# Weight-block sums by accumulating DMA, and a rearranged end, in an encoder layer on one NeuronCore

## Chip, cores, metric

One core of a Trainium2 chip runs one encoder layer for two request groups. The metric is the time of one execution on the device in microseconds (us); lower is better. Three runs of the kernel before are the base.

## Reference

```python
def encoder_trunk(x, mem, ...):          # prompt: 512 tokens, sample: 1024 tokens, D = 1024
    x = layer_norm(x, ln_in_g, ln_in_b)
    x = layer_norm(ALPHA * x + token_mixer(x, ...), ln1_g, ln1_b)
    x = layer_norm(ALPHA * x + memory_cross_attention(x, mem, ...), ln2_g, ln2_b)
    x = layer_norm(ALPHA * x + squared_relu_mlp(x, w_up, w_down), ln3_g, ln3_b)
    return x

def squared_relu_mlp(x, w_up, w_down):   # w_up: 1024 x 4096, w_down: 4096 x 1024
    return jnp.square(jax.nn.relu(x @ w_up)) @ w_down
```

All is float32. The change lies in the MLP of the two groups, in the norm behind it, and in nothing ahead of it.

## The kernel before

Every float32 product is made of three matmuls: an operand is split into a rounded high part (a copy on ACT into float32r) and the rest (a subtraction on GpSimd or DVE), and high x high, high x low, low x high are added in PSUM. `V`, `A`, `G`, `T`, `S` are the queues of DVE (VectorE), ACT (ScalarE), GpSimd (POOL), TensorE and SP, which issues all DMAs. A scheduler orders each queue when the program is built; buffers come from rings (`SLOT`: `qt`, `pt`, `gb`, `kv` two of 128x1024 each, `q` seven of 128x512, `cpr` two; `wh` and `wl` three of 128x1024 each; `act` six of 128x4096), so a load waits until the tile that held its buffer is used up.

**MLP of the prompt.** 32 steps f. Each loads 128 columns of `w_up` and 128 rows of `w_down` (`col_block`, `down_weights`), splits them (ACT, GpSimd), makes the hidden block (`up`: 24 matmuls, relu, square, split) and adds its product with the `w_down` rows to the four token tiles (`down`: 24 matmuls, eight DVE additions from PSUM). Beside it `left` makes ready, for the sample group, the left operands of the next stage: four blocks per product, each a sum or difference of two blocks of the activations or one alone, split and stored to `sa` in DRAM.

**MLP of the sample group.** Both matrix products are done as 2 x 2 blocks with seven products instead of eight (Strassen). `PRODUCTS[i]` names for each product its left blocks, its right (weight) blocks and where the result is added or subtracted; `UP` and `DOWN` are the orders of the seven. A step of an up product (16 a product) loads one or two 128x512 weight blocks (`up_block`, 256 KB each), combines two of them on DVE into `cpr`, splits (`right`, with the subtraction on GpSimd here), does 12 matmuls and adds the bank to one or two hidden blocks. `left_load` fetches a product's four left tiles from `sa` some half a product ahead. A step of a down product combines and splits a hidden block (left) and a `w_down` block (right), both subtractions on DVE, and does 12 matmuls for four token tiles; behind a product its four banks are added to the accumulators `accs`. `finish(0)` normalizes the upper 512 rows behind product 1, `finish(1)` the lower 512 behind the last product:

```python
        if i == 1:
            finish(0)
    finish(1)
```

Of the kernel before, what the change touches and what calls it, by code (L numbers as in the profile page):

```python
# [36 lines left out]
def tile_encoder_layer(ctx: ExitStack, tc: tile.TileContext, d, outs):  # L37
# [818 lines left out]
    for t in range(4):  # L856
# [16 lines left out]
    UP, DOWN = (5, 3, 2, 4, 1, 7, 6), (3, 5, 4, 2, 7, 1, 6)  # L873


    def left(i):
        blk = lambda b, k: X2[1 + b[0]][:, 4 * b[1] + k]
        what = PRODUCTS[i][0]
        for k in range(4):
            x = blk(what[0], k)  # L880
            if len(what) > 1:
                y = slot("cpr")
                V.tensor_tensor(y, x, blk(what[2], k), op=what[1])
                x = y
            t = slot("kv", dt=F32R)
            A.activation(t[:, 0:512], x, AF.Copy)
            V.tensor_sub(t[:, 512:1024], x, f32(t[:, 0:512]))
            S.dma_start(sa[i - 1][k], f32(t).rearrange("p (j c) -> p j c", j=2))
# [65 lines left out]
    def right(what, load, low, tag=None):  # L954
# [75 lines left out]
    for n, i in enumerate(DOWN):  # L1030
# [33 lines left out]
        if i == 1:  # L1064
            finish(0)
# [65 lines left out]
```

## Time and profile before

| | us |
|---|---|
| median of three runs (2437.79 to 2443.6) | 2439.3 |
| the profiled execution | 2432.93 |
| its span, first to last instruction | 2431.2 |
| TensorE busy | 2321.2 (95%) |
| MLP of the prompt, first to last `down` addition (L925) | 1415.8 to 1773 |
| up products, sample | about 1780 to 2086 |
| down products, sample | 2086 to 2412 |

The chip's profiler records each instruction with its engine and line; "PE" is TensorE, "DVE" VectorE, "ACT" ScalarE, "POOL" GpSimd. PEclk is the share of TensorE's full clock that was granted. A wait is put down to the instruction that ended last before it. Window rows read: stretch, its length, then busy us and (x count) of PE, PEld (weight loads), DVE, ACT and POOL, then PEclk, the mean busy share of the 16 DMA engines, and GB/s.

### The profile page before, as it was taken

How to read it: one execution, taken by the hardware profiler on the slowest of the kernel's cores; microseconds unless marked ns; L12 is line 12 of the kernel's file. 1: busy time of each engine (PE TensorE's matmuls, PEld its weight loads, DVE VectorE, ACT ScalarE, POOL GpSimd, SP SyncE). 2: the span in 40 equal slices, each digit the busy share in tenths (PEclk: the TensorE clock that was granted, in tenths of full speed). 3: DMA queues.
4: the chain of work that ended last, by engine and by line, in shares of the span. 5: the costliest groups of instructions: out<-in, count | busy, mean ns of one | idle time of the engine just before them, and what ended most of it. 6: DMA issues, size and time to landing. Idle time of an engine off the chain costs nothing.

```text
span 2431.2 us, 33241 instructions
## 1 busy us (share of the span) xinstructions
PE 2321.2 (95%) x11128; PEld 1916.6 (79%) x11128; DVE 1667.1 (69%) x3294; ACT 1034.1 (43%) x2181; POOL 910.0 (37%) x798
## 2 busy tenths in 40 slices
PE   8989999999999999999989989999999999999995
PEld 6868778898888787778878876788888877888873
DVE  6266545666656776658576679666655799887997
ACT  4346644666545634434233334333354222344432
POOL 7555442121234125333244444454475445100013
PEclk9999999999999999999999999999999999999998
DMA  9676345444444543435325366433376677634553
GB/s 323 199 191 174 85 119 131 118 115 101 94 119 116 168 130 104 139 113 173 108 92 188 101 205 242 131 98 93 100 242 180 192 240 219 208 125 147 189 170 119
DMA packets 394043, 371.00 MB, mean 153 GB/s; under 512 B 72976, under 2 KB 302352, under 8 KB 393872
## 3 DMA queue, kind: packets, MB, share of 16 engines
q1 hardware_dynamic: 393872, 368.88, 50.7%
q8 instruction: 88, 1.44, 0.2%
q14 instruction: 83, 0.68, 0.1%
HBM read 290.75 MB, written 52.97 MB: 141 GB/s over the span
## 4 chain that ended last, share of the span: by engine, by line
PE 38%; DVE 9%; DMA 4%; issue 3%; POOL 2%; ACT 1%; POOLq 0%; SPq 0%; DVEq 0%; ACTq 0%
PE pj L128 5%; PE pj L129 5%; PE pj L130 5%; DVE cpr L960 2%; PE s L128 2%; PE s L130 2%; PE s L129 2%; PE t L128 2%; PE t L130 2%; PE t L129 2%; PE t L1045 1%; PE t L1046 1%; PE t L1047 1%; DVE h L1001 1%; DMA q<-in_w_up_dram 1%
## 5 line engine op out<-in xcount | busy, mean ns | idle before, releaser
L106 POOL TENSOR_TENSOR wl<-wraw,wh 128x512 fp32r<-128x512 f32 x144 | 196.6, 1378 | 262.8 <-ACT wh L105 240.3
L960 DVE TENSOR_TENSOR cpr<-q 128x512 f32<-128x512 f32 x160 | 148.8, 931 | 47.4 <-DMA q<-in_w_up_dram 19.2
L155 POOL TENSOR_TENSOR lnst<-lnst,mhalf 128x1 f32<-128x1 f32 x48 | 51.6, 1078 | 342.5 <-DVE lnst L154 339.6
L432 ACT ACTIVATE q<-q,st 128x256 f32<-128x256 f32 (+3 forms) x256 | 138.2, 545 | 74.9 <-DVE st L431 72.0
L963 ACT ACTIVATE wh<-cpr 128x512 fp32r<-128x512 f32 x160 | 100.3, 627 | 161.5 <-DVE cpr L960 140.2
L105 ACT ACTIVATE wh<-wraw 128x512 fp32r<-128x512 f32 x144 | 87.9, 629 | 182.3 <-DMA wraw<-in_w_up_dram 50.3
L478 DVE TENSOR_TENSOR pt<-t,pt 128x512 fp32r<-128x512 f32 x160 | 105.4, 671 | 86.5 <-ACT pt L477 85.9
L964 POOL TENSOR_TENSOR wh<-cpr,wh 128x512 fp32r<-128x512 f32 x80 | 114.4, 1431 | 115.7 <-ACT wh L963 115.7
L296 POOL TENSOR_TENSOR wl<-wraw,wh 128x256 fp32r<-128x256 f32 x128 | 95.5, 771 | 153.5 <-ACT wh L295 141.8
L912 POOL TENSOR_TENSOR wl<-wraw,wh 128x512 fp32r<-128x512 f32 x64 | 87.4, 1378 | 122.4 <-ACT wh L911 122.3
L477 ACT ACTIVATE pt<-t 128x512 fp32r<-128x512 f32 x160 | 89.5, 583 | 87.9 <-PE o L490 84.6
L490 PE MATMUL o<-pt,tok 128*128 128x256 f32 (+3 forms) x560 | 114.3, 315 | 5.7 <-ACT q L496 4.3
L925 DVE TENSOR_TENSOR tok<-tok,s 128x512 f32<-128x512 f32 x124 | 83.5, 681 | 41.1 <-PE s L130 41.0
L118 POOL TENSOR_TENSOR wl<-wraw,wh 128x512 fp32r<-128x512 f32 x48 | 62.9, 1324 | 124.9 <-ACT wh L117 124.7
L128 PE MATMUL pj<-x20h,wh 128*128 128x512 f32 x256 | 102.1, 399 | 7.1 <-ACT wh L105 7.0
L925 DVE TENSOR_TENSOR tok<-tok,t 128x512 f32<-128x512 f32 x124 | 83.1, 682 | 31.7 <-PE t L130 31.6
L130 PE MATMUL pj<-x20h,wl 128*128 128x512 f32 x256 | 102.1, 399 | 2.2 <-POOL wl L106 2.1
L129 PE MATMUL pj<-x20l,wh 128*128 128x512 f32 x256 | 101.7, 397 | 0.0
L1040 ACT ACTIVATE wh<-wraw 128x512 fp32r<-128x512 f32 x80 | 50.6, 633 | 119.0 <-issue 40.8
L474 PE MATMUL t<-ident,q 128*128 128x128 f32 x624 | 94.9, 274 | 2.2 <-DVE pt L478 1.0
L490 PEld LDWEIGHTS o<-pt,tok 128*128 128x128 f32 x560 | 83.5, 192 | 11.3 <-ACT q L496 6.2
L428 DVE CUSTOM_DVE_ANT_0 q<-s,gb 128x256 f32<-128x256 f32 (+2 forms) x160 | 67.9, 466 | 27.4 <-PE s L449 21.6
(478 smaller groups left out, 7545.3 us busy)
## 6 DMA issues: line engine op xcount, KB each, us to landing
q<-in_w_up_dram SPq DMA_DIRECT2D x192, 256.0 KB
q<-in_w_down_dram SPq DMA_DIRECT2D x192, 256.0 KB
wraw<-in_w_in_dram SPq DMA_DIRECT2D x96, 256.0 KB
wraw<-in_w_up_dram SPq DMA_DIRECT2D x64, 256.0 KB
wraw<-in_w_down_dram SPq DMA_DIRECT2D x64, 256.0 KB
sa<-kv SPq DMA_DIRECT2D x28, 512.0 KB
kv<-in_c_rope_dram SPq DMA_DIRECT2D x24, 512.0 KB
hd<-qt SPq DMA_DIRECT2D x96, 128.0 KB
```

Of the source, the lines that this page charges most:

```text
L106: G.tensor_sub(wl[:, sl], r, f32(wh[:, sl]))
L128: T.matmul(out, lh[k], rh[k], start=(k == 0), stop=False, skip_group_check=True)
L129: T.matmul(out, lh[k], rl[k], start=False, stop=False, skip_group_check=True)
L130: T.matmul(out, ll[k], rh[k], start=False, stop=(k == n - 1), skip_group_check=True)
L296: G.tensor_sub(dl, src, f32(dh))
L432: A.activation(p, p, AF.Exp, bias=nm, accum_out=den)
L478: V.tensor_sub(lo[:, 0:x], t[:, 0:x], f32(hi[:, 0:x]))
L490: T.matmul(o[:, q0:q0 + n], v(c, h), part[:, x:x + n], start=(done == 0 and part is hi), stop=(done == total - 1 and part is lo), skip_gro ...
L925: V.tensor_add(x, x, q)
L960: V.tensor_tensor(y, x, z, op=what[1])
L963: A.activation(t[:, 0:512], x, AF.Copy)
L964: low.tensor_sub(t[:, 512:1024], x, f32(t[:, 0:512]))
```

## The change

Four parts. (1) Where a product's two weight blocks are added, `right` loads the first into a `q` buffer through SP and lets GpSimd issue a second DMA that adds its block to that buffer; the DVE addition goes. Signs in `PRODUCTS` are changed so that all right operands but product 1's are sums (its difference stays on DVE, L970 in the new file). In the up products the split's subtraction goes from GpSimd to DVE (L964, L976 in the new file). (2) `left` works on one block a step in 28 steps instead of four in 7, and the prompt's MLP loads whole 512 KB tiles of weights into `qt` and `pt`. (3) `DOWN` becomes (3, 5, 4, 7, 1, 6, 2). The last product goes over tokens 0 to 383 first (three banks) and keeps its weight splits in `act` buffers (`kept`), then over the last 128 tokens. (4) The upper rows' statistics are taken behind products 5 and 1, and their norms stand inside the last product's loop; the lower rows' norms follow their banks tile by tile.

```diff
-    def layer_norm(x, g, b, spread=0):
+    def layer_norm(x, g, b, spread=0, st=None):
-        st = sb.tile([P, 16], F32, name="lnst", bufs=2)
-        V.bn_stats(st[:, 0:6], x[:, 0:512])
-        V.bn_stats(st[:, 6:12], x[:, 512:1024])
+        if st is None:
+            st = sb.tile([P, 16], F32, name="lnst", bufs=2)
+            V.bn_stats(st[:, 0:6], x[:, 0:512])
+            V.bn_stats(st[:, 6:12], x[:, 512:1024])
...
-        3: (((0, 0),), ((0, 1), SUB, (1, 1)), (((0, 1), ADD), ((1, 1), ADD))),
+        3: (((0, 0),), ((0, 1), ADD, (1, 1)), (((0, 1), ADD), ((1, 1), ADD))),
...
-    UP, DOWN = (5, 3, 2, 4, 1, 7, 6), (3, 5, 4, 2, 7, 1, 6)
+    UP, DOWN = (5, 3, 2, 4, 1, 7, 6), (3, 5, 4, 7, 1, 6, 2)
...
     def down_weights(f):
         hi, lo = (x.rearrange("p (j c) -> p j c", j=2) for x in w_parts())
+        raw = w_raw(wdn[f * P:(f + 1) * P].rearrange("p (j c) -> p j c", j=2), "pt")
         for ch in range(2):
-            raw = w_raw(wdn[f * P:(f + 1) * P, None, ch * 512:(ch + 1) * 512])[:, 0]
-            A.activation(hi[:, ch], raw, AF.Copy)
-            G.tensor_sub(lo[:, ch], raw, f32(hi[:, ch]))
+            A.activation(hi[:, ch], raw[:, ch], AF.Copy)
+            G.tensor_sub(lo[:, ch], raw[:, ch], f32(hi[:, ch]))
...
-        w, dn = col_block(wup, f * P), down_weights(f)
+        w, dn = col_block(wup, f * P, "qt"), down_weights(f)
         down(up(w), dn, f == 0)
-        if 3 <= f < 10:
-            left(UP[f - 3])
+        if 3 <= f < 31:
+            left(UP[(f - 3) // 4], (f - 3) % 4)
...
+    def transfer(out, src, onto):
+        if onto is None:
+            S.dma_start(out, src)
+        else:
+            G.dma_start(out, src, accum_op=ADD)
...
         x = load(what[0])
-        if len(what) > 1:
+        if len(what) > 1 and what[1] == ADD:
+            load(what[2], x)
+        elif len(what) > 1:
             z = load(what[2])
             y = slot("cpr")
             V.tensor_tensor(y, x, z, op=what[1])
             x = y
...
-            wh_, wl_ = (x.rearrange("p (k c) -> p k c", k=4) for x in right(what, up_block(f), G))
+            wh_, wl_ = (x.rearrange("p (k c) -> p k c", k=4) for x in right(what, up_block(f), V))
...
+    def left_parts(lw, c, t0, t1):
+        n = (t1 - t0) * P
+        x = hidden(lw[0], c)[:, t0 * P:t1 * P]
+        if len(lw) > 1:
+            y = wp.tile([P, 512], F32, name="wraw", tag="wraw", bufs=2)[:, 0:n]
+            V.tensor_tensor(y, x, hidden(lw[2], c)[:, t0 * P:t1 * P], op=lw[1])
+            x = y
+        a = wp.tile([P, 1024], F32R, name="wh", tag="wh")
+        A.activation(a[:, 0:n], x, AF.Copy)
+        V.tensor_sub(a[:, 512:512 + n], x, f32(a[:, 0:n]))
...
+    for n, i in enumerate(DOWN[:-1]):
...
+        if i in (5, 1):
+            for t in range(4):
+                stats(0, t, 1 if i == 5 else 0)
...
+    for c in range(16):
+        if c % 8 == 0:
+            kept.append([act.tile([P, 8, 512], F32R, name="kept", tag="act") for _ in range(2)])
+        rs = right(rw, down_block(c), V, dst=[k[:, c % 8] for k in kept[c // 8]])
+        chunk(banks[0:3], left_parts(lw, c, 0, 3), rs, c)
+        if c % 4 == 3:
+            finish(0, c // 4, 1)
+    for t in range(3):
+        collect(into, t, banks[t])
+    for c in range(16):
+        chunk(banks[3:4], left_parts(lw, c, 3, 4), [k[:, c % 8] for k in kept[c // 8]], c)
+    for t in range(4):
+        if t == 3:
+            collect(into, 3, banks[3])
+        finish(1, t, 2 if t == 3 else 1)
```

Up to the prompt's MLP every queue stands as before. Three places behind that show what moved. The first is DVE's queue in the middle of the burst of `left` before (L883 combines two blocks, L887 is a split's subtraction into `kv`, L925 an addition to a token tile, L901 and L904 belong to `up`):

```order
L901 TENSOR_TENSOR cpr<-cpr 128x512
L887 TENSOR_TENSOR kv<-cpr,kv 128x512
L904 TENSOR_TENSOR q<-cpr,q 128x512
L925 TENSOR_TENSOR tok<-tok,s 128x512
L887 TENSOR_TENSOR kv<-xt_13867,kv 128x512
L883 TENSOR_TENSOR cpr<-xt_12957,xt_13867 128x512
L887 TENSOR_TENSOR kv<-xt_13867,kv 128x512
L901 TENSOR_TENSOR cpr<-cpr 128x512
L925 TENSOR_TENSOR tok<-tok,t 128x512
L925 TENSOR_TENSOR tok<-tok,s 128x512
L925 TENSOR_TENSOR tok<-tok,t 128x512 x2
L887 TENSOR_TENSOR kv<-xt_13867,kv 128x512
```

and the same queue in a step of the change (the lines are now L884, L888, L926, L902, L905):

```order
L884 TENSOR_TENSOR cpr<-xt_12957,xt_13867 128x512
L926 TENSOR_TENSOR tok<-tok,s 128x512
L926 TENSOR_TENSOR tok<-tok,t 128x512
L902 TENSOR_TENSOR cpr<-cpr 128x512
L926 TENSOR_TENSOR tok<-tok,s 128x512
L888 TENSOR_TENSOR kv<-cpr,kv 128x512
L905 TENSOR_TENSOR q<-cpr,q 128x512
L926 TENSOR_TENSOR tok<-tok,s 128x512
```

Four splits for `kv` among a few additions have become one among a step's additions.

The second is GpSimd's queue from the end of the prompt's norms through all products of the sample group, before (L155 and L170 are norms, L964 the splits' subtractions; `qt` are upper rows):

```order
L170 TENSOR_TENSOR tok<-tok,gb 128x1024
L964 TENSOR_TENSOR wh<-q,wh 128x512 x4
L964 TENSOR_TENSOR wh<-cpr,wh 128x512 x16
L964 TENSOR_TENSOR wh<-q,wh 128x512 x16
L964 TENSOR_TENSOR wh<-cpr,wh 128x512 x64
L155 TENSOR_TENSOR lnst<-lnst,mhalf 128x1 x2
```

and now (L960 issues an accumulating DMA, L157 and L172 are norms):

```order
L960 DMA q<-in_w_up_dram 128x4x128
L172 TENSOR_TENSOR tok<-tok,gb 128x1024
L960 DMA q<-in_w_up_dram 128x4x128 x62
L960 DMA q<-in_w_down_dram 128x512 x60
L157 TENSOR_TENSOR st<-st,mhalf 128x1 x4
L960 DMA q<-in_w_down_dram 128x512 x4
L172 TENSOR_TENSOR qt<-qt,q 128x512 x2
```

All subtractions have left this queue, and 128 DMAs stand in it, the last four of them behind the upper rows' first norm operations.

The third is DVE's queue at the end. Before, the last banks (L1057) and the lower rows' norms follow the last split (L964):

```order
L964 TENSOR_TENSOR wh<-cpr,wh 128x512
L1057 TENSOR_TENSOR gb<-gb,pj 128x512 x2
L152 BN_STATS lnst<-gb 128x6
L1057 TENSOR_TENSOR kv<-kv,s 128x512 x2
L152 BN_STATS lnst<-gb 128x6
L153 BN_AGGR lnst<-lnst 128x2 x2
L154 TENSOR_SCALAR lnst<-lnst 128x1
L159 SCALAR_TENSOR_TENSOR gb<-gb,lnst,g_21726 128x512 x2
```

Now the first three tiles' banks (L1072) and norms (L153 to L161) stand among the second pass's small combinations and splits (L1052, L1056):

```order
L1056 TENSOR_TENSOR wh<-wraw,wh 128x128
L1052 TENSOR_TENSOR wraw<-tok,h_17336 128x128
L1072 TENSOR_TENSOR gb<-gb,pj 128x512 x4
L1072 TENSOR_TENSOR kv<-kv,s 128x512 x2
L153 BN_STATS lnst<-gb 128x6
L1056 TENSOR_TENSOR wh<-wraw,wh 128x128
L154 BN_STATS lnst<-gb 128x6
L1056 TENSOR_TENSOR wh<-wraw,wh 128x128
L153 BN_STATS lnst<-gb 128x6
L154 BN_STATS lnst<-gb 128x6
L1052 TENSOR_TENSOR wraw<-tok,h_17336 128x128
```

Three of the four lower tiles are now collected and normalized ahead of the last matmuls, not behind them.

## Rows read from the trace of the kernel before

**Rows 1.** The page: TensorE's busy time, its share of the span, instructions.

```profile
PE 2321.2 (95%) x11128; PEld 1916.6 (79%) x11128; DVE 1667.1 (69%) x3294; ACT 1034.1 (43%) x2181; POOL 910.0 (37%) x798
```

**Rows 2.** Windows: MLP burst, MLP later, up twice, down twice, after the last matmul.

```profile
1440.00:1530.00 90.00, 77.21 (x302) 59.16 (x301) 77.09 (x107) 38.45 (x65) 38.05 (x26) 0.92 0.71 248
1600.00:1760.00 160.00, 160.00 (x697) 130.24 (x696) 102.24 (x146) 51.41 (x86) 78.07 (x58) 1.00 0.33 98
1780.00:1940.00 160.00, 160.00 (x700) 131.20 (x699) 96.36 (x123) 68.83 (x120) 92.31 (x64) 1.00 0.70 210
1940.00:2060.00 120.00, 114.11 (x484) 92.41 (x484) 115.48 (x130) 25.54 (x41) 59.30 (x41) 0.97 0.77 230
2060.00:2340.00 280.00, 279.61 (x1230) 230.42 (x1229) 244.39 (x385) 114.52 (x196) 10.04 (x6) 1.00 0.53 172
2340.00:2412.00 72.00, 57.30 (x230) 44.41 (x228) 62.01 (x107) 24.66 (x40) 20.61 (x8) 0.95 0.38 128
2412.00:2431.20 19.20, 0.00 (x0) 0.00 (x0) 13.22 (x28) 4.11 (x6) 9.81 (x8) 0.63 0.27 109
```

**Rows 3.** Waits from 1390 to 1530 us: total us, times, longest.

```profile
ACT wh L105 <- DMA wraw<-in_w_up_dram: 20.2, 14, 3.8
ACT kv L886 <- DMA sa<-kv: 18.9, 14, 4.1
...
PE pj L128 <- ACT wh L105: 6.9, 3, 5.4
```

**Rows 4.** The chain that ended last, from 1700 us: start, us, what.

```profile
2009.35 1.79 DVE cpr L960
2012.38 1.78 DVE cpr L960
...
2129.97 0.68 PE t L1045 x3
2132.69 0.68 PE t L1045 x3
...
2305.04 0.68 PE t L1045 x3
```

**Rows 5.** Lines L960 and L964: count, ns of one (least/median/most), first and last start.

```profile
L960 DVE TENSOR_TENSOR cpr<-q x160: 665/691/1793, 1794.4 to 2403.1; 128x512 f32<-128x512 f32 x160
...
L964 POOL TENSOR_TENSOR wh<-cpr,wh x80: 1278/1298/1806, 1803.2 to 2075.6; 128x512 fp32r<-128x512 f32 x80
```

**Rows 6.** Windows in an up and a down product; SP's issue of up blocks.

```profile
1912.00:1948.00 36.00, 34.63 (x153) 28.39 (x152) 35.62 (x45) 6.96 (x11) 14.24 (x11) 1.00 0.59 171
2132.00:2168.00 36.00, 36.00 (x161) 29.80 (x160) 30.12 (x49) 15.15 (x26) 0.00 (x0) 1.00 0.40 125
...
L971 SPq DMA_DIRECT2D q<-in_w_up_dram x192: 367/430/1977, 1753.6 to 2065.8; - x192
```

**Rows 7.** Waits of TensorE from 2085 to 2431 us, the longest.

```profile
PE pj L1046 <- DVE wh L964: 13.8, 8, 4.3
```

**Rows 8.** Timeline of the end: start, us, engine, line, operation, count.

```profile
2411.56 0.39 PE L1047 MATMUL s<-wh 128*128 128x512 f32 x1
...
2412.43 1.26 DVE L1057 TENSOR_TENSOR kv<-kv,s 128x512 f32<-128x512 f32 x2
...
2418.49 0.69 DVE L151 BATCH_NORM_STATS2 lnst<-kv 128x6 f32<-128x512 f32 x1
...
2419.09 0.68 DVE L152 BATCH_NORM_STATS2 lnst<-kv 128x6 f32<-128x512 f32 x1
...
2422.55 1.41 DVE L159 SCALAR_TENSOR_TENSOR kv<-kv,lnst,g 128x512 f32<-128x512 f32 x2
...
2424.54 0.69 DVE L168 TENSOR_TENSOR kv<-kv,g 128x512 f32<-128x512 f32 x1
```

**Rows 9.** Line L170, GpSimd's bias additions of the last norms: count, ns of one.

```profile
L170 POOL TENSOR_TENSOR pt<-pt,g x2: 4859/6048/7237, 2382.3 to 2387.1; 128x512 f32<-128x512 f32 x2
L170 POOL TENSOR_TENSOR gb<-gb,g x2: 1262/1536/1809, 2417.9 to 2419.7; 128x512 f32<-128x512 f32 x2
```

More of the change, by code (lines that the diff above doesn't have):

```diff
@@ L872, in tile_encoder_layer, with left @@
     }
-    UP, DOWN = (5, 3, 2, 4, 1, 7, 6), (3, 5, 4, 2, 7, 1, 6)
-    def left(i):
-        blk = lambda b, k: X2[1 + b[0]][:, 4 * b[1] + k]
+    UP, DOWN = (5, 3, 2, 4, 1, 7, 6), (3, 5, 4, 7, 1, 6, 2)
+    def left(i, k):
+        blk = lambda b: X2[1 + b[0]][:, 4 * b[1] + k]
         what = PRODUCTS[i][0]
-        for k in range(4):
-            x = blk(what[0], k)
-            if len(what) > 1:
[L882 to L888, printed above, removed]
+        x = blk(what[0])
+        if len(what) > 1:
+            y = slot("cpr")
+            V.tensor_tensor(y, x, blk(what[2]), op=what[1])
+            x = y
+        t = slot("kv", dt=F32R)
+        A.activation(t[:, 0:512], x, AF.Copy)
+        V.tensor_sub(t[:, 512:1024], x, f32(t[:, 0:512]))
+        S.dma_start(sa[i - 1][k], f32(t).rearrange("p (j c) -> p j c", j=2))
     toks[0] = [slot("tok") for _ in range(4)]
@@ L961, in right, with load @@
             x = y
[L962 to L965 removed]
+        if dst is None:
+            t = wp.tile([P, 1024], F32R, name="wh", tag=tag or ("wh", "wl")[next(ring) % 2])
+            dst = t[:, 0:512], t[:, 512:1024]
+        A.activation(dst[0], x, AF.Copy)
+        low.tensor_sub(dst[1], x, f32(dst[0]))
+        return dst
     def up_block(f):
[L968 to L969 removed]
+        def load(b, onto=None):
+            r = slot("q", 512) if onto is None else onto
             c0 = b[1] * 2048 + f * P
[L971 to L972 removed]
+            transfer(r.rearrange("p (k c) -> p k c", k=4),
+                     wup[b[0] * 512:(b[0] + 1) * 512, c0:c0 + P].rearrange("(k p) c -> p k c", p=P), onto)
             return r
@@ L1013, in down_block, with load @@
     def down_block(c):
-        def load(b):
-            r = slot("q", 512)
+        def load(b, onto=None):
+            r = slot("q", 512) if onto is None else onto
             row = b[0] * 2048 + c * P
-            S.dma_start(r, wdn[row:row + P, b[1] * 512:(b[1] + 1) * 512])
+            transfer(r, wdn[row:row + P, b[1] * 512:(b[1] + 1) * 512], onto)
             return r
@@ L1021, in tile_encoder_layer, with stats, finish, chunk @@
     done = set()
-    g3 = None
-    def finish(h):
-        for t in range(4):
-            layer_norm(accs[h][t], [g3[:, 0], g3[:, 1]], [g3[:, 2], g3[:, 3]], 1 if t % 2 else 2)
-            row = 512 * h + t * P
-            S.dma_start(outs[1][0, row:row + P], accs[h][t])
-    for n, i in enumerate(DOWN):
+    stat = {}
+    def stats(h, t, ch):
+        if (h, t) not in stat:
+            stat[h, t] = sb.tile([P, 16], F32, name="st", bufs=4)
+        V.bn_stats(stat[h, t][:, 6 * ch:6 * ch + 6], accs[h][t][:, ch * 512:(ch + 1) * 512])
+    def finish(h, t, spread):
+        layer_norm(accs[h][t], g3, b3, spread, stat.get((h, t)))
+        row = 512 * h + t * P
+        S.dma_start(outs[1][0, row:row + P], accs[h][t])
+    def left_parts(lw, c, t0, t1):
[4 more added lines that the diff above has]
+            V.tensor_tensor(y, x, hidden(lw[2], c)[:, t0 * P:t1 * P], op=lw[1])
+            x = y
+        a = wp.tile([P, 1024], F32R, name="wh", tag="wh")
+        A.activation(a[:, 0:n], x, AF.Copy)
+        V.tensor_sub(a[:, 512:512 + n], x, f32(a[:, 0:n]))
+        return [(a[:, j * P:(j + 1) * P], a[:, 512 + j * P:512 + (j + 1) * P]) for j in range(t1 - t0)]
+    def chunk(banks, ls, rs, c):
+        for o, (lh, ll) in zip(banks, ls):
+            T.matmul(o, lh, rs[0], start=(c == 0), stop=False)
+            T.matmul(o, lh, rs[1], start=False, stop=False)
+            T.matmul(o, ll, rs[0], start=False, stop=(c == 15))
+    def collect(into, t, o):
+        for b, op in into:
+            x = accs[b[0]][t][:, b[1] * 512:(b[1] + 1) * 512]
+            if (b, t) not in done:
+                done.add((b, t))
+                V.scalar_tensor_tensor(x, x, ALPHA, o, op0=ALU.mult, op1=op)
+            else:
+                V.tensor_tensor(x, x, o, op=op)
+    for n, i in enumerate(DOWN[:-1]):
         lw, rw, into = PRODUCTS[i]
```

60 lines of the change are left out of this document (16 added, 44 removed).

## Prediction

> **What bounds the kernel now.** I read the page first: TensorE is busy 95% of 2431.2 us [rows 1], so an engine that is merely slow costs nothing; only the places where TensorE loses matmuls count. The busy figure hides them, because a matmul at a lower clock is also busy. So I read the windows by stage and counted matmuls against the pace of an undisturbed stretch of the same stage [rows 2]:
>
> - MLP of the prompt: 697 in 160 us is 0.2296 us each. From 1440 to 1530 there are 302, worth 69.3 us of 90: **20.7 us lost**, at a mean granted clock of 0.92, so part of it is matmuls at the lower of the two levels (1.2 of 2.4 GHz) after idling.
> - Up products: 700 in 160 us, 0.2286 each. From 1940 to 2060 there are 484, worth 110.6 of 120: about **9 us lost**, at 0.97; DVE is busy 115.48 of the 120.
> - Down products: 1230 in 280 us, 0.2276 each. From 2340 to 2412 there are 230, worth 52.4 of 72: **19.6 us lost**, clock 0.95, DVE busy 62 of 72.
> - After the last matmul: **19 us** without any.
>
> That is about 69 us; the rest is matmul work that the change keeps (1536 in the MLP and 1344 in each set of products, by the loops). The waits say what is late in the MLP stretch: weight splits on ACT for weight loads (20.2 us), ACT in `left` for stores to `sa` that free a `kv` buffer (18.9 us), and TensorE then for those splits [rows 3]. At the end TensorE waits for DVE's L964, 13.8 us in 8 waits [rows 7].
>
> **MLP stage.** Four blocks of `left` followed each of seven steps f; now one follows each of 28. A step of TensorE is 48 x 0.2296 = 11.0 us. DVE starts a 128x512 operation every 0.60 us where nothing hinders it, though each row says 0.69 [rows 8]. A step has 8 additions, a square and a subtraction, 10 x 0.60 = 6.0 us; the burst added 28 subtractions and 20 additions over 7 steps, 4.1 us, so 10.1 of 11.0, before any two-input operation is slowed by GpSimd (1.79 us where L960 meets L964, 0.69 alone [rows 4, 5]). Spread, it is 1.0 us: 7.0 of 11.0. The stores go from four to one per step, so a `kv` buffer is no longer waited for ahead of the splits in ACT's queue. Weights are loaded as whole 512 KB tiles into two `qt` and two `pt` buffers instead of 256 KB pieces through two `wraw` buffers; that addresses the 20.2 us, for the same bytes. So I take 18 of the 20.7 back; bounds 21 and 10 (the first steps fill new buffers, and the spread blocks also meet GpSimd's splits). New risk: `left_load(0)` needs `qt` and `pt`, which the MLP's weights now hold almost to its end. In the new order the last `left` block stands 19 additions, over two steps, before DVE's last MLP addition, and the ring of three split buffers has the last weights split about a step before TensorE ends, so the 4 x 512 KB (1.7 us each at the price below) fit into that step; I charge nothing and keep 5 us in the bounds.
>
> **Up products.** L960 goes from 160 to 32 DVE additions or subtractions (product 1 in both stages keeps its SUB); GpSimd loses its 112 subtractions (L964) in this stage to DVE and issues 64 accumulating DMAs here, 64 more in the down products. A step of TensorE is 12 matmuls, 2.72 us [rows 4]. Where DVE met GpSimd it took 3.03 us a step (two starts of L960) [rows 4]. Without GpSimd reading beside it, the fullest step (product 1, or one with two targets) has four DVE operations, 4 x 0.60 = 2.4 us, and the others three: below 2.72. The 9 us lost go; I take 7, because the second level of waits below may take a little, bounds 9 and 0.
>
> **What an accumulating DMA costs** no row shows: before has none, and none issued by GpSimd. Two prices are open. (a) Engine time: a 256 KB up block in 512 B pieces takes 0.59 x 36 us / (171 GB/s x 36 us / 262144 B) = 0.90 us of all 16 engines, a down block in 2 KB pieces 0.40 x 36 / 17.2 = 0.84 [rows 6]. Lower bound: the same as the load that it replaces, 0.90. Upper bound from rows: it also moves the sum out of and into SBUF, as a second transfer would, 1.80. With the other block and the left operands (4 x 512 KB per product at the down price: 0.42 per step) a step needs 2.2 to 3.1 us of the DMA engines in the up stage, and 1.7 to 2.5 in the down stage, against 2.72. (b) Issue on GpSimd: below, SP's 0.43 us for the same shape [rows 6]; above, GpSimd's own slowest 128x512 operation here, 6.05 us in the mean, when it was kept waiting beside a full DVE [rows 9]; near 1.3 to 1.5 when it ran freely [rows 5, 9]. I take values below 2.72 for both: from 1800 us to product 6 of the down products GpSimd has nothing else to do, and DVE no longer fills every slot.
>
> What covers a moderate excess is the lead: 7 `q` buffers and 6 split pairs (3 in the down stage) stand between the DMA and TensorE, 6 to 13 steps, 16 to 35 us. It refills in products 5 and 2, which load one block. An excess of 0.4 us a step is 6 us over a product of 16 steps and 13 over the two last up products, which lie together: covered. The added latency of two transfers in a row is covered by the same lead.
>
> The Trainium skill, "Collectives: The Full Stack", Part 3, says that a reducing DMA is slower than a copy not for the addition but since it reads two sources through one ring, and measures a ratio of 1.93. No run here shows it yet. By that figure the up step needs 0.42 + 0.90 + 1.74 = 3.06 us; it is the upper bound above, which came from the rows.
>
> **The end.** Product 2 (one weight block, DVE's lighter kind) now comes last, tokens 0 to 383 first and the last 128 in a second pass over the kept splits; the upper rows' statistics and norms move into product 6. The sixth product starts at 2305.0 [rows 4] in both. From there DVE has, by the new order, 92 operations of 128x512 at 0.60 (55.2), 14 L161 at 0.70 (9.8; a pair is 1.41 [rows 8]), 32 of 384 columns (15.0 at three quarters of 0.60 and a little) and 32 of 128 (6.4, a third of 0.60, both estimates from that row), 14 small ones (1.4): 87.8 us, against 384 x 0.2276 = 87.4 for TensorE. GpSimd's 14 bias additions make DVE wait: 14 x 1.1 = 15 us; a lead of three steps takes 8 back. So TensorE loses about 8, most of it in the second pass, where the first three token tiles' collecting and norms stand between the small splits; before it lost 19.6. After the last matmul DVE has 1.26 for the two sums, 1.2 statistics, 0.3, 1.4 and 1.4 for scale, bias: 5.6; from the end of L168 to the end of the span before it was 6.0 [rows 8]. That is 11.6 against 19.2. Together 11 + 7 = 18; bounds 27 (no contention) and 8 (every second-pass split late).
>
> **Sum.** 18 + 7 + 18 = 43 us. The profiled execution took 2432.9, the median of the three runs is 2439.3: 6.4 us apart, as runs differ. The terms are of the profiled one (2390 by it); I subtract them from the median: **2396**. Without a rival the bounds are 2439 - 57 = 2382 and 2439 - 13 = 2426, with the 5 us of the MLP's end.
>
> **Rivals.**
> 1. *The DMA engines bind the up products* (3.1 us a step, and the lead smaller than counted): at worst 64 x 0.38 = 24 us given back, 2420. For it: they are at 0.77 over 1940 to 2060 [rows 2], and a sum read twice takes more. Against: products 5 and 2 refill the lead.
> 2. *Slower: GpSimd takes longer than a step to issue one.* The accumulating products lie in six stretches, four of one product and two of two; a lead of 16 us covers the first of each. An excess of 1.1 us, 3.8 us a DMA, leaves 4 x (16 x 1.1 - 16) + 2 x (32 x 1.1 - 16) = 45 and outweighs the 43: from there it decides. At 4.0 us it is 70 and 2466; at the upper row's 6.05, 330 and some 2726. For it: GpSimd was held 4.9 to 7.2 us beside a full DVE [rows 9]. Against: that was a two-input operation. The Trainium skill, "SBUF — State Buffer", on the trap of DVE blocking a DMA from GpSimd, says that GpSimd writes the descriptors itself and is shut out while DVE runs a two-port operation, 0.62 us becoming 3.1; of `tensor_tensor`, DVE's only frequent operation here, it infers that it does not shut them out. By 3.1 each such step would be 0.4 over, which the lead covers; no row here shows it.
> 3. *Given back*: TensorE stalls at the MLP's end for `left_load(0)`, and DVE binds the second pass fully, some 40 us in all: 2432 to 2446.
>
> **Chances.** Forecast 0.57 (2382 to 2410), still better 0.03, rival 1 0.20 (2405 to 2428, so faster too), rival 3 0.07, rival 2 0.13. Range for 8 in 10: 2380 to 2436, leaving out rival 2 and the edge of rival 3. A difference under 0.3% (7 us) can't be told from none: faster 0.80, within 0.07, slower 0.13.
>
> **What would show it.** In the new trace: the MLP stretch at TensorE's pace and clock 1.00, no waits for `sa` stores; L976 on DVE at 0.69 in the up stage; matmul counts of 219 per 50 us through products 4, 1, 7 and 6; DMA share there below 1; GpSimd's issue rows below 2.7 us; last matmul to end near 12 us. It is wrong if splits on ACT wait for `q` for whole products (rivals 1 and 2, told apart by DMA share and GpSimd's issue time), or if the first up product waits for `qt` and `pt`.

## The result, and the profile after

The changed kernel takes **2400.0 us** (median of four runs, 2399.4 to 2402.3) against 2438.6 before (2429.1 to 2443.6): a ratio of 0.9848, interval 0.9817 to 0.9879. The forecast was 2396, 2380 to 2436. The profiled execution took 2400.22, span 2398.4.

The time is near the forecast, but one of the forecast's three terms is far from what came. Cut at the first matmul of each stage, the two traces give these lengths in us (worked out from the matmul records; "down 6" and "down 7" are the sixth and seventh down product, "behind" is what follows the last matmul):

```
           MLP     up   down 1-5  down 6  down 7  behind   span
before   381.5  317.5    218.6     43.5    63.6    19.2   2431.2
after    364.5  308.1    217.8     47.0    65.0     9.7   2398.4
```

The MLP gave 17.0 (18 forecast), the up products 9.4 (7), the end, which is the last three columns, 126.3 to 121.7: 4.6 where 18 were forecast. Line numbers are those of each run's own file, so the same operation can stand at another line from run to run.

From the page of after (part 1, then the queue that GpSimd issues, with packets, MB and share of 16 engines, then its issues with the median from issue to landing):

```profile
PE 2313.8 (96%) x11128; PEld 1911.1 (80%) x11128; DVE 1599.5 (67%) x3304; ACT 1028.7 (43%) x2200; POOL 906.0 (38%) x820
...
q0 software_dynamic: 43008, 33.56, 9.9%
...
q<-in_w_up_dram POOLq DMA_DIRECT2D x64, 256.0 KB, 8.2
q<-in_w_down_dram POOLq DMA_DIRECT2D x64, 256.0 KB, 6.0
```

The windows of after, as in [rows 2], cut finer at the end:

```profile
1440.00:1530.00 90.00, 89.02 (x385) 71.75 (x384) 63.13 (x92) 31.37 (x56) 47.94 (x32) 1.00 0.45 141
1600.00:1760.00 160.00, 159.81 (x690) 128.75 (x689) 120.36 (x182) 57.54 (x103) 79.38 (x52) 1.00 0.49 152
1780.00:1940.00 160.00, 160.00 (x701) 131.28 (x700) 102.78 (x166) 57.64 (x101) 37.66 (x30) 1.00 0.96 218
1940.00:2060.00 120.00, 120.00 (x525) 98.13 (x524) 91.40 (x148) 28.99 (x46) 48.36 (x40) 1.00 1.18 239
2060.00:2276.00 216.00, 216.00 (x954) 178.66 (x953) 159.62 (x257) 91.47 (x158) 40.69 (x47) 1.00 0.75 180
2276.00:2324.00 48.00, 45.78 (x198) 36.58 (x197) 43.26 (x73) 23.18 (x39) 21.92 (x18) 1.00 0.63 139
2324.00:2366.00 42.00, 36.65 (x152) 28.92 (x150) 34.06 (x60) 16.77 (x33) 6.28 (x4) 0.96 0.42 138
2366.00:2389.00 23.00, 16.62 (x41) 10.18 (x40) 19.99 (x48) 7.13 (x18) 11.50 (x9) 0.63 0.17 68
2389.00:2398.40 9.40, 0.00 (x0) 0.00 (x0) 5.34 (x10) 0.72 (x1) 0.92 (x1) 0.70 0.14 57
```

The burst's stretch now holds 385 matmuls, 88.4 us of 90 at 0.2296 (302 before). The up stage runs at its pace (525 in 120 us; 484 before) although the DMA share reads 1.18. All that is left to lose lies at the end: at 0.2276 a matmul, 198, 152 and 41 are worth 45.1, 34.6 and 9.3 us of 48, 42 and 23: 2.9, 7.4 and 13.7 lost, 24.0 together. What TensorE waited for there:

```profile
PE s L1063 <- DVE wh L1056: 5.1, 3, 2.4
PE pj L1061 <- ACT wh L1055: 4.5, 1, 4.5
PE t L1062 <- DVE wh L976: 2.2, 3, 1.4
PE s L1061 <- ACT wh L1055: 1.1, 2, 0.8
PE pj L1063 <- DVE wh L1056: 0.8, 1, 0.8
```

The waits are 13.7 us; most of the rest is matmuls at the lower of the two clocks behind them (0.63 granted from 2366). (L1061 to L1063 are the three matmuls of a step, L1055 and L1056 split the left block, L976 the weights.) DVE's timeline at the start of the second pass shows why the waits are there, and TensorE's what they do:

```profile
2363.06 0.29 DVE L1052 TENSOR_TENSOR wraw<-tok,h 128x128 f32<-128x128 f32 x1
2363.93 2.48 DVE L1072 TENSOR_TENSOR gb<-gb,pj 128x512 f32<-128x512 f32 x4 [0.57 <-PE pj L1063]
2366.33 1.27 DVE L1072 TENSOR_TENSOR kv<-kv,s 128x512 f32<-128x512 f32 x2
2367.52 0.68 DVE L153 BATCH_NORM_STATS2 lnst<-gb 128x6 f32<-128x512 f32 x1
2368.13 0.27 DVE L1056 TENSOR_TENSOR wh<-wraw,wh 128x128 fp32r<-128x128 f32 x1
```

```profile
2365.77 0.39 PE L1062 MATMUL s<-kept,wh 128*128 128x512 f32 x1
2368.45 0.53 PE L1063 MATMUL s<-kept,wh 128*128 128x512 f32 x1 [2.29 <-DVE wh L1056]
2368.79 0.62 PE L1061 MATMUL s<-kept,wh 128*128 128x512 f32 x1
2369.20 0.63 PE L1062 MATMUL s<-kept,wh 128*128 128x512 f32 x1
```

A split of 128 columns takes DVE 0.27 us, but it stands behind six collecting additions and a statistic, 4.2 us, while a step of the second pass is three matmuls, 0.68 us. TensorE waits, and then starts a matmul every 0.4 us instead of every 0.23.

### The profile page after: what moved, and what is told of

It reads as the page before. It is cut to its first block, busy times and chain, and to the rows that moved or that the text cites. A ratio compares the mean times of both kernels' runs of the same rounds, so it can differ in the third digit from the quotient of the medians.

```text
span 2398.4 us, 33111 instructions
## 1 busy us (share of the span) xinstructions
PE 2313.8 (96%) x11128; PEld 1911.1 (80%) x11128; DVE 1599.5 (67%) x3304; ACT 1028.7 (43%) x2200; POOL 906.0 (38%) x820
## 3 DMA queue, kind: packets, MB, share of 16 engines
q0 software_dynamic: 43008, 33.56, 9.9%
## 5 line engine op out<-in xcount | busy, mean ns | idle before, releaser
L106 POOL TENSOR_TENSOR wl<-wraw,wh 128x512 fp32r<-128x512 f32 x80 | 105.9, 1338 | 183.5 <-ACT wh L105 167.3
L975 ACT ACTIVATE wh<-q 128x512 fp32r<-128x512 f32 x176 | 110.0, 625 | 132.7 <-DMA q<-in_w_up_dram 84.4
L976 DVE TENSOR_TENSOR wh<-q,wh 128x512 fp32r<-128x512 f32 x176 | 126.3, 720 | 56.8 <-ACT wh L975 56.8
L960 POOL DMA_DIRECT2D q<-in_w_up_dram x64 | 84.1, 1463 | 182.2 <-DVE h L1013 74.8
L913 POOL TENSOR_TENSOR wl<-pt,wh 128x512 fp32r<-128x512 f32 x64 | 91.6, 1451 | 119.0 <-ACT wh L912 118.7
L960 POOL DMA_DIRECT2D q<-in_w_down_dram x64 | 56.4, 956 | 203.4 <-DMA q<-in_w_down_dram 92.2
L106 POOL TENSOR_TENSOR wl<-qt,wh 128x512 fp32r<-128x512 f32 x64 | 101.7, 1609 | 51.6 <-ACT wh L105 43.7
L118 POOL TENSOR_TENSOR wl<-wraw,wh 128x512 fp32r<-128x512 f32 x48 | 62.3, 1314 | 127.8 <-ACT wh L117 127.8
L926 DVE TENSOR_TENSOR tok<-tok,t 128x512 f32<-128x512 f32 x124 | 82.8, 679 | 37.3 <-PE t L130 37.3
L926 DVE TENSOR_TENSOR tok<-tok,s 128x512 f32<-128x512 f32 x124 | 83.8, 679 | 29.7 <-PE s L130 29.5
L1055 ACT ACTIVATE wh<-wraw 128x512 fp32r<-128x512 f32 (+2 forms) x96 | 53.1, 557 | 106.9 <-issue 45.5
L105 ACT ACTIVATE wh<-wraw 128x512 fp32r<-128x512 f32 x80 | 48.0, 627 | 104.1 <-DMA wraw<-in_w_xq_dram 27.2
```

The lines of the kernel that those rows point to most:

```text
L106: G.tensor_sub(wl[:, sl], r, f32(wh[:, sl]))
L926: V.tensor_add(x, x, q)
L960: G.dma_start(out, src, accum_op=ADD)
L975: A.activation(dst[0], x, AF.Copy)
L976: low.tensor_sub(dst[1], x, f32(dst[0]))
```

## The experiments

The stage lengths of all runs, made as above, come first, since most verdicts are read from them; each run's text names its row. They are of one execution each: the MLP of e2_acc, in which nothing was changed, took 384.5 us and that of the kernel before 381.5, so a difference of 3 us in that column shows nothing.

```
                    MLP     up   down 1-5  down 6  down 7  behind
e1_mlp            365.0  316.5    219.9     43.5    64.7    19.2
e2_acc            384.5  308.1    218.2     43.5    52.8    19.6
e3_no_acc         367.1  308.1    220.4     58.5    57.4     9.5
e4_old_end        363.9  308.1    217.7     43.5    54.3    19.6
e5_sub_pool       364.9  344.8    217.8     46.0    65.3     9.7
e6_sum_dve        364.5  308.1    219.2     59.0    57.2     9.5
e8_plain          365.3  308.1    217.8     44.6    65.7     9.7
e9_store          364.6  308.1    217.8     46.9    64.5     9.4
e10_bias_dma      365.3  308.1    217.8     48.9    56.2     9.4
e11_new_end       366.7  308.1    217.8     55.2    47.2    23.5
e12_old_end_dve   365.0  308.1    218.6     43.5    63.8    19.2
e13_late_norms    364.8  308.1    217.8     50.4    52.8    16.7
```

**The parts alone and in pairs.** "MLP" is part 2 of the change, "DMA" part 1, "end" parts 3 and 4. The kernel before took 2435.7 beside these four.

MLP alone:

```diff
-        if 3 <= f < 10:
-            left(UP[f - 3])
+        if 3 <= f < 31:
+            left(UP[(f - 3) // 4], (f - 3) % 4)
```

> The kernel before with only the prompt's MLP changed (one block of left a step in 28 steps, whole 512 KB weight tiles through qt and pt). My theory: the burst of four blocks a step was the whole of the 20.7 us lost from 1440 to 1530, so this alone takes 18 to 21 us off the time of the kernel before (2438.6), about 2419, and the up and down stages lose what they lost before (9, 19.6 and 19.2 behind the last matmul). Rival: the stage only hides a debt; the first up product then waits for left_load(0), and 5 us or less is gained, 2434.

Measured: 2418.7, ratio 0.9936 (0.9920 to 0.9952). That is 17.0 below the kernel before, a little under the 18 to 21 of the theory; the MLP takes 365.0, 16.5 less, and the rest stays. The theory holds, and no debt moves into the up products. The two halves of this part, the spread blocks and the whole weight tiles, were not run apart.

DMA alone:

```diff
-            z = load(what[2])
-            V.tensor_tensor(y, x, z, op=what[1])
+            load(what[2], x)
...
-            wh_, wl_ = (x.rearrange("p (k c) -> p k c", k=4) for x in right(what, up_block(f), G))
+            wh_, wl_ = (x.rearrange("p (k c) -> p k c", k=4) for x in right(what, up_block(f), V))
```

> The kernel before with only the accumulating DMAs, the moved signs and the up split's subtraction on DVE; the MLP and the order of the down products are as before. My theory: the up products lose nothing more (9 us back), and the old end loses less, because product 6, which stands last, has three DVE operations a step instead of four (before 19.6 us lost there); together 9 to 20 us, 2419 to 2430. The 19 us behind the last matmul stay. Rival: the DMA does what DVE did at the same place in the chain, and nothing but the 9 us or less comes: 2430 to 2438.

Measured: 2411.5, ratio 0.9904 (0.9882 to 0.9925): 24 us, more than either expected. Up loses nothing (9.4 less), and the seventh product of the old order, product 6, takes 52.8 for 63.6. These two are 20.2; where the other 4 of the medians lie its trace, whose MLP is 3 longer, does not show.

MLP and end, without the DMA:

```diff
-        if len(what) > 1 and what[1] == ADD:
-            load(what[2], x)
-        elif len(what) > 1:
+        if len(what) > 1:
...
-            wh_, wl_ = (x.rearrange("p (k c) -> p k c", k=4) for x in right(what, up_block(f), V))
+            wh_, wl_ = (x.rearrange("p (k c) -> p k c", k=4) for x in right(what, up_block(f), G))
```

> The changed kernel without its first part: weight blocks summed on DVE again and the up split's subtraction on GpSimd; MLP and end as changed. My theory: 9 us are lost again in the up products, and about 10 in the last two down products, where DVE has 16 additions of 0.60 us more in product 6 on top of the upper rows' norms: 2400 + 19, about 2419. Rival: the end is bound by the norms and small splits alone, and only the 9 us come back: 2409. A second rival, that the first part is worth nothing: 2400.

Measured: 2417.8, ratio 0.9930 (0.9907 to 0.9952). The time is the theory's, but its trace shows only the second half of it: down 6 takes 58.5, up 308.1 as in after. That profile is of the fastest of six runs (2406.5 to 2425.1); what the others lost, and where, no trace shows. And the end gave nothing here: 2417.8 with it, 2418.7 without.

MLP and DMA, with the old end:

```diff
-    UP, DOWN = (5, 3, 2, 4, 1, 7, 6), (3, 5, 4, 7, 1, 6, 2)
+    UP, DOWN = (5, 3, 2, 4, 1, 7, 6), (3, 5, 4, 2, 7, 1, 6)
```

> The changed kernel with the old end (old order of the down products, norms behind products 1 and 6, one pass for the last product); accumulating DMAs and MLP as changed. My theory: the time behind the last matmul goes from about 10 back to 19 us, and the stretch before it, in which the changed kernel still loses about 20 us, loses 10 to 20 here: 2400 to 2412. Rival: the new end is worth the full 18 us that I forecast: 2418.

Measured: 2396.3 (2396.1 to 2396.6), ratio 0.9842 (0.9827 to 0.9856). Both expectations miss: the old end is not slower, but 3.7 us faster. From down 6 on it takes 117.4, the new one 121.7.

**What in the DMA part gives the time.** The kernel before took 2436.8 beside these four. First the subtraction back on GpSimd:

```diff
-            wh_, wl_ = (x.rearrange("p (k c) -> p k c", k=4) for x in right(what, up_block(f), V))
+            wh_, wl_ = (x.rearrange("p (k c) -> p k c", k=4) for x in right(what, up_block(f), G))
```

> The changed kernel with the up split's subtraction on GpSimd again, beside the accumulating DMAs (112 subtractions move from DVE to GpSimd; nothing else). My theory: what the up products won came from GpSimd no longer reading beside DVE, not from the DMA's sum. Then times spread by 10 us or more from run to run again, as in the kernels so far that subtract there (2406 to 2425), and the median is 5 to 15 us above 2400. Rival: DVE has one addition less per step, so it has room for slowed operations (two or three of 1.3 us fit 2.72 us or nearly), and the time stays at 2400 with a spread under 4 us.

Measured: 2440.1 (2433.1 to 2447.4), ratio 1.0014 (1.0000 to 1.0029): this one operation on the other engine undoes the whole gain. Up takes 344.8. GpSimd's groups and TensorE's waits in it:

```profile
L976 POOL TENSOR_TENSOR wh<-q,wh 128x512 fp32r<-128x512 f32 x88 | 157.1, 2115 | 11.0 <-ACT wh L975 9.5 <-DMA q<-in_w_up_dram 1.5
L960 POOL DMA_DIRECT2D q<-in_w_up_dram x64 | 97.1, 1637 | 48.1 <-DMA q<-in_w_up_dram 41.5 <-POOL wh L976 2.9 <-issue 1.4
```

```profile
PE t L130 <- POOL wh L976: 10.2, 7, 2.8
PE pj L130 <- POOL wh L976: 5.5, 5, 2.3
PE s L130 <- POOL wh L976: 4.8, 3, 3.4
```

A step of GpSimd is 2.12 + 1.64 = 3.76 us with 2.72 to spend, and while it waits for the first block of a sum, the subtractions queue behind. That is what rival 2 described, a step of GpSimd longer than one of TensorE, here brought about by a second job on that queue. Rival 2's count, with a lead of 16 us, would make of 1.04 us a step some 19 us in the up products; 36.7 were lost, and by the records the splits had no lead left (0.0 us) when product 7 began. Both expectations were too mild; the runs lie 14 us apart, as the first had it.

Then the sums back on DVE and the subtraction left there:

```diff
-        if len(what) > 1 and what[1] == ADD:
-            load(what[2], x)
-        elif len(what) > 1:
+        if len(what) > 1:
```

> The changed kernel with the weight blocks summed on DVE again and the up split's subtraction left on DVE: no accumulating DMA, and no GpSimd work beside DVE in the up products. My theory: four DVE operations of 0.60 us, 2.4 of 2.72 us a step, so the up products lose nothing (308 us as in the changed kernel) and the runs lie within 5 us; but product 6 of the down products, with the sixteen sums and behind it the norms, loses about 11 us more, as without the whole first part (58.5 against 47.0 us): 2408 to 2412. Rival: DVE binds the up products at 0.69 to 0.72 us an operation, 2.8 to 2.9 a step, and 10 more are lost there: 2420.

Measured: 2403.3 (2399.6 to 2407.0), ratio 0.9863 (0.9845 to 0.9881). Its windows over the up stage and the last two products:

```profile
1744.90:2053.00 308.10, 308.10 (x1345) 252.32 (x1344) 260.14 (x416) 108.05 (x181) 16.15 (x8) 1.00 0.75 223
2272.20:2331.20 59.00, 47.00 (x193) 37.26 (x192) 58.14 (x92) 25.88 (x42) 34.91 (x12) 0.91 0.49 157
2331.20:2388.40 57.20, 50.23 (x193) 37.78 (x191) 46.91 (x100) 22.57 (x48) 11.51 (x9) 0.88 0.25 87
```

In the up stage DVE carries everything, 260 of 308 us, and TensorE loses nothing: no accumulating DMA is needed there. In down 6 DVE is full (58.14 of 59.0), and it takes 12.0 us longer than in after, as expected, but down 7 is 7.8 shorter, so that 4.2 are left of the 11 expected, and the time is below the 2408 to 2412 of the theory; the runs lie 7.4 apart, not 5.

This run and the one without any of the first part (2417.8, 2406.5 to 2425.1) differ in one thing, the engine of the up split's subtraction, and lie 14.5 us apart (ratios 0.9930 and 0.9863, whose intervals do not meet). So with this end most of what the first part is worth comes from moving the subtraction to DVE; the accumulating DMA on top of it gives 3.3 us, 2403.3 to 2400.0, and there the intervals overlap.

Then the price of adding itself:

```diff
-            G.dma_start(out, src, accum_op=ADD)
+            G.dma_start(out, src)
```

> The changed kernel with the second DMA writing over the first block instead of adding to it (so the right operands are single blocks, and that part of the computation is left out); same bytes from DRAM, same queue, same waits. My theory: TensorE hides the whole cost of adding, so the time stays at 2400 within 3 us; the packets of GpSimd's queue fall from 65 to about 27 ns for 512 B and from 178 to 201 to about 84 ns for 2 KB, and the issue on GpSimd stays at 1.28 us. Rival: the adding costs time somewhere, by contention with the other loads, and without it the kernel is 5 us or more faster.

Measured: 2403.6 and 2402.9 in two runs: not faster, so the adding costs nothing that TensorE sees. From its page, and GpSimd's issues in it and in after, from 1760 to 2100:

```profile
q0 software_dynamic: 10240, 33.56, 4.5%
...
q<-in_w_up_dram POOLq DMA_DIRECT2D x64, 256.0 KB, 4.4
```

```profile
L960 POOL DMA_DIRECT2D q<-in_w_up_dram x64 | 48.1, 752 | 206.7 <-DVE wh L976 71.9 <-DVE h L1013 69.3 <-DMA q<-in_w_up_dram 40.3
```

```profile
L960 POOL DMA_DIRECT2D q<-in_w_up_dram x64 | 84.1, 1463 | 182.2 <-DVE h L1013 74.8 <-DMA q<-in_w_up_dram 45.6 <-DVE wh L976 36.3
```

The expectation on packets missed: without adding, the queue moves the same bytes in 10240 packets, not 43008, and the issue halves, 0.75 for 1.46 us.

**The end.** The last of the four moved the upper rows' stores:

```diff
-        S.dma_start(outs[1][0, row:row + P], accs[h][t])
+        (S if h else G).dma_start(outs[1][0, row:row + P], accs[h][t])
```

> The changed kernel with the four stores of the upper rows' output issued by GpSimd, which computes their last step, and not by SP, whose queue also issues the weight loads of the last product. My theory: the 4.9 us stall of TensorE at 2326, a store in SP's queue that waits for GpSimd's addition with weight loads behind it, goes, and with it some of the matmuls at the lower clock behind it: 5 to 8 us, 2392 to 2395. Rival: DVE's queue of norms and splits binds there anyway and the stall comes back as a wait for it: 2398 to 2400.

Measured: 2402.0 (2397.4 to 2402.7), ratio 0.9854 (0.9837 to 0.9871). The rival's mechanism is right, though its time (2398 to 2400) is a little short: the 4.5 us wait goes to 1.2, one for DVE's splits grows from 0.8 to 4.4, and down 6 and 7 take 111.4 for 112.0.

```profile
PE pj L1063 <- DVE wh L1056: 4.4, 3, 2.0
...
PE pj L1061 <- ACT wh L1055: 1.2, 1, 1.2
```

The kernel before took 2435.8 beside three of the last four, and 2435.4 beside the mended end. First the bias rows by accumulating DMA:

```diff
-                G.tensor_add(xi, xi, b[i])
+        G.dma_start(accs[h][t], bass.AP(tensor=src.tensor, offset=src.offset, ap=[[0, P], [1, D]]), accum_op=ADD)
```

> The changed kernel with the norms' last step (adding the bias row) done by an accumulating DMA for the four upper tiles and the first three lower ones, in place of GpSimd's 14 additions; the upper rows' stores are GpSimd's too. My theory: those additions hold up DVE's two-input operations in the last two products, where the changed kernel loses 24.6 us; without them 8 to 15 us come back: 2385 to 2392. Rival: what is lost there comes from DVE's order of work (small splits behind norms and collecting), and nothing changes: 2397 to 2403.

Measured: 2397.8 (2394.0 to 2399.5), ratio 0.9839 (0.9818 to 0.9859). Down 6 and 7 take 105.1, 6.9 less than in after and 6.3 less than in the run before, which has the stores on GpSimd too: not nothing, and below the theory's 8 to 15. The time lies in the rival's range, 2.2 below after and 4.2 below the run before, with overlapping intervals (in this trace the MLP starts 5 us later than in after, ahead of anything changed).

Then all splits of the last product in its first pass, and the upper norms in down 6:

```diff
-        chunk(banks[0:3], left_parts(lw, c, 0, 3), rs, c)
+        ls.append(left_once(lw, c))
+        chunk(banks[0:3], ls[c][0:3], rs, c)
...
-        chunk(banks[3:4], left_parts(lw, c, 3, 4), [k[:, c % 8] for k in kept[c // 8]], c)
+        chunk(banks[3:4], ls[c][3:4], [k[:, c % 8] for k in kept[c // 8]], c)
...
+            if i == 6 and c % 4 == 3:
+                finish(0, c // 4, 3)
```

> The changed kernel with another end: the upper rows' norms stand in product 6, where DVE has 28.8 us of splits in 43.6; product 2's left blocks are combined and split once for all four token tiles (the last 128 columns into buffers of their own), so its second pass has no work on DVE but collecting and norms; bias rows by accumulating DMA as in the run before. My theory: DVE's 86 us of operations from product 6 on fit TensorE's 87.2 with the lead of three steps, the last two products take 88 to 95 us instead of 112, and the end behind the last matmul stays at 9.7: 2377 to 2384. Rival: at 99 per cent of the time DVE binds, as it does in the changed kernel, and 10 to 15 us are lost there again: 2388 to 2396.

Measured: 2405.8 (2397.7 to 2410.5), ratio 0.9876 (0.9856 to 0.9897). Both expectations miss: down 7 falls to 47.2, but down 6 takes 55.2, the two together 102.4 where the theory had 88 to 95, and the end behind them is 23.5. Two rows of its timeline, of ACT in down 6 and of DVE near the last matmul (2384.8):

```profile
2303.13 1.34 ACT L168 ACTIVATE pt<-pt,st 128x512 f32<-128x512 f32 x2 [2.61 <-POOL st L157]
...
2379.66 2.48 DVE L1078 TENSOR_TENSOR gb<-gb,pj 128x512 f32<-128x512 f32 x4 [4.72 <-PE pj L1069]
```

A norm's step on ACT waits for GpSimd's power, queued among DMA issues, with splits behind it; and the second pass, free of DVE now, had been scheduled into the first, so that three tiles' collecting starts 5 us before the last matmul.

Both mended:

```diff
-        chunk(banks[3:4], ls[c][3:4], [k[:, c % 8] for k in kept[c // 8]], c)
+        chunk(banks[3:4], ls[15 - c][3:4], [k[:, (15 - c) % 8] for k in kept[1 - c // 8]], c)
...
-            if i == 6 and c % 4 == 3:
+            if i == 6 and c in (3, 6, 9, 12):
```

> The run with the new end, mended at the two places where its trace lost time: the second pass goes through the sixteen steps from the last to the first, so that it can't start before the first pass ends (before, its matmuls were mixed into the first pass, and the norms of the three token tiles came behind the last matmul); and each upper tile's norm is tied to step 3, 6, 9 or 12 of product 6, with all GpSimd powers ahead of it, instead of all four norms in its first third. My theory: what was lost is order, not capacity, so product 6 takes 44 to 47 us (55.2 before the mending), product 2 45 to 50, and the end behind the last matmul 10 to 13: 2378 to 2387. Rival: DVE has no room in these two products whatever the order, and the sum of the three stays at 115 or more: 2392 to 2400.

Measured: 2402.2 (2396.9 to 2404.2), ratio 0.9864 (0.9843 to 0.9885); 50.4, 52.8 and 16.7 are 119.9. The time misses both ranges, but the sum is above the rival's 115: the loss moves among the three places and stays, 5.4 us above the 114.5 of the run that only moved the bias rows. That DVE has no room isn't shown by it, though, for DVE is busy 42.7 of 50.5 and 39.2 of 52.8 us there:

```profile
2282.00:2332.50 50.50, 46.22 (x194) 37.09 (x193) 42.73 (x82) 25.49 (x45) 17.09 (x20) 0.97 0.90 210
2332.50:2385.30 52.80, 46.43 (x193) 36.67 (x191) 39.19 (x81) 18.66 (x43) 3.59 (x5) 0.97 0.24 69
```

TensorE's waits of 10.6 us there are put down mostly to splits on ACT, and ACT's to late weight loads and once to GpSimd's power (L1070 and L1100 split the left block, L979 the weights, L170 is a norm's step, L1048 the power):

```profile
PE pj L1076 <- ACT wh L1100: 4.9, 2, 4.1
PE t L1076 <- ACT wh L1070: 4.0, 1, 4.0
...
ACT kept L979 <- DMA q<-in_w_down_dram: 15.3, 10, 5.5
...
ACT qt L170 <- POOL st L1048: 4.0, 1, 4.0
```

What made those loads late no run shows.

Last, the old end with DVE sums:

```diff
-        if len(what) > 1 and what[1] == ADD:
-            load(what[2], x)
-        elif len(what) > 1:
+        if len(what) > 1:
```

> The kernel with the old end that was tried first (accumulating DMAs, spread MLP), with the weight blocks summed on DVE instead; the up split's subtraction stays on DVE. My theory: the accumulating DMA is worth nothing in the up products (the run with DVE sums lost nothing there) and is worth 9 to 11 us where product 6 stands last, since DVE then has four operations a step beside the norms: 2405 to 2408. Rival: it is worth nothing there either: 2396 to 2399.

Measured: 2408.0 (2400.5 to 2413.9), ratio 0.9883 (0.9864 to 0.9902). The theory holds: down 7 takes 63.8 here. Its window, and that of the same product with the DMA sums:

```profile
2325.10:2388.90 63.80, 49.82 (x193) 38.20 (x191) 54.10 (x94) 21.19 (x34) 20.50 (x8) 0.92 0.35 116
```

```profile
2320.40:2374.70 54.30, 47.38 (x193) 36.46 (x191) 46.55 (x81) 20.50 (x34) 19.46 (x17) 0.97 0.56 129
```

So the accumulating DMA is worth 9.5 us in the product where DVE is short (54.10 us busy beside 46.55), 11.7 by the medians with this end, and nothing in the up products, where the subtraction is on DVE too and the stage takes 308.1 either way. From down 6 on the old end with DVE sums takes 126.5 us, and the new one (e6_sum_dve) 125.7: without the DMA the two ends are nearly alike. The step before it in this order, from the MLP alone (2418.7) to this run, is the subtraction's move with the signs: 10.7 us, with intervals that do not meet.

## Why the prediction was right, and where it was not

**MLP, 18.** Right in mechanism and size: 17.0, and 16.5 alone. ACT's waits for stores to `sa` from 1390 to 1530 fell from 18.9 to 4.8 us, though the forecast's sign was none:

```profile
ACT kv L887 <- DMA sa<-kv: 4.8, 2, 4.3
```

The new risk did not come: between 1740 and 2080 TensorE has no wait, and the up stage takes 308.1, as short as in any run. Whether the spread blocks or the whole weight tiles gave it stays open.

**Up, 7.** The size (9.4) is just above the upper bound of 9. The reason given, that GpSimd no longer reads beside DVE, is the half that counts: with the sums on DVE as well nothing is lost in the stage, and moving the subtraction alone is worth 14.5 us of the median with the new end and 10.7 with the old. The 36.7 us lost with the subtraction beside the DMAs are another matter, GpSimd's own full queue. What the reason leaves open is the run without the DMA, which in its fastest execution had the old division of work and lost nothing in the up products; so GpSimd beside DVE does not cost 9 us each time, and where those us lie no trace shows.

**The accumulating DMA.** Issue: 1.46 us in the mean, 2.30 at most, below 2.72 as taken. Engine time: 9.9% of 2398.4 us over 128 DMAs is 1.85 us each, 2.08 for an up block (512 packets at 65 ns, over 16 engines, from the DMA records), above the upper bound of 1.80. An up step then needs 0.42 + 0.90 + 2.08 = 3.40 of 2.72 us, where the forecast had taken a value below 2.72 and a DMA share below 1: this term was mis-sized. By rival 1's count the excess of 0.68 us a step is 22 us over the two last up products, to be paid out of the lead. It was not paid: TensorE lost nothing at a share of 1.18, and by the records of after the splits ended 8.5 us before their matmuls at the start of product 7 and 8.8 at the end of product 6, and never less than 6.0 in between. A share above 1 says that packet times overlap on an engine; so the count, which takes them for time that excludes other packets, was wrong as well. That the two errors cancelled is luck. On the ratio of 1.93 that the Trainium skill gives in "Collectives: The Full Stack", Part 3, for a reducing against a copying transfer: the shares in the profile make it 1.85 to 0.84 (4.5% of 2401.8 over 128), 2.2, between an accumulating and a plain DMA of the same bytes. Rival 2's count has a slip too: in the new orders products 7 and 6 of the up stage and product 3 of the down stage follow one another, so the accumulating products lie in five stretches, one of three products, and 3.8 us a DMA would have cost 61 us by its own formula, not 45.

**The end, 18.** This is the step that failed. The forecast had TensorE lose "about 8" and 11.6 behind it; it lost 24.6 (112.0 less 384 x 0.2276) and 9.7. GpSimd's additions fit their price: a 128x512 split of DVE in the last product takes 0.69 us in the median and up to 1.77 beside them, 1.1 more; 15 less 8 of lead is 7, and without them 6.3 came back. Missing was the rest, some 17: the sum compared DVE's 87.8 us with TensorE's 87.4 over two products, as if the order did not matter. The trace of after shows what that leaves out: DVE works its queue in order, the lead is three steps, and a clump of norms and collecting in front of a small split becomes a wait of TensorE, with matmuls at the lower clock behind it. That this is the whole of the 17 is read from the waits and not shown by a run: the two runs that changed the order moved the loss (125.9 and 119.9 us from down 6 on, for 121.7 in after and 114.5 with the bias rows alone moved, as theirs are too) and did not take it away.

Nor does the new order give the 4.6 that came. From down 6 on before takes 126.3; with the MLP changed and the subtraction and the sums on DVE the old end takes 126.5 and the new one 125.7, and with the accumulating DMA 117.4 and 121.7. So the DMA is worth 9.1 us in the old end and 4.0 in the new, and the new order gives 0.8 without it, which one trace of each can't tell from none, and costs 4.3 with it (by the medians it gives 4.7, with overlapping runs, and costs 3.7).

**The sum.** Terms of 17.0, 9.4 and 4.6, with 1.8 in other stages and the rounding, are the 32.8 between the two spans, where 43 were forecast: by the profiled execution the forecast was 2390, and 2400.2 came. The median moved by 38.5, because before's profiled execution lay 5.6 below its median and after's lies on its own. Taking the terms off the median made the forecast look better than its terms, which is luck; why before's runs lie apart by 14 us and after's by 3 stays open.

**Best version.** The old end with the two other parts, 2396.3, lies 3.7 us below the changed kernel, with no overlap of their runs, but that is 0.15%, and the ratios' intervals overlap. With the bias rows by DMA the new end is the shorter of the two by its trace (114.5 for 117.4), and 1.5 us longer by the medians.

## What to carry to other kernels

Run the parts of a change alone: three terms of a right sum can hide one that is four times too large. A DMA that adds is worth what the engine that it relieves is short of, stage by stage, and it needs a queue with no other work that can make it wait or wait for it. When a change moves two things, move them back one at a time: here the subtraction's move gave 14.5 us with the new end and 10.7 with the old, and the DMA after which the change is named 3.3 and 11.7. Where a busy engine feeds the critical one in order, compare clumps with the lead, not only totals with totals.

## What was not expected of the hardware

- The mean busy share of the DMA engines reached 1.18 over 120 us at 239 GB/s, with no loss on TensorE. Over 1800 to 2050 it was 1.05 there, and 0.76 with plain writes of the same bytes.
- An accumulating transfer stays in small packets (43008 for 33.56 MB, 512 B taking 65 ns where SP's plain ones take 27), plain ones from the same queue went in 10240; issue of an up block 1.46 against 0.75 us, landing 8.2 against 4.4.
- GpSimd's issue was not held up by DVE's two-input operations: 1.46 us in the mean beside a DVE busy 91 of 120 us. By the records the 27 of the 64 issues that had DVE at work for three quarters of their time or more took 1.42, the 8 that had it for less than a quarter 1.53. The 3.1 us that the Trainium skill, "SBUF — State Buffer", section "A bandwidth-pool intuition that's wrong (but worth ruling out)", gives for a GpSimd that DVE shuts out did not appear in the mean of any run, which agrees with what the page infers for `tensor_tensor` in "Who interferes with whom". Beside GpSimd's own subtractions the mean was 1.64.
